# Attention scores of two heads: from split fp32r products to fp32 products issued side by side

## The chip, the cores and the metric

The kernel runs on one core of one Trainium2 chip. The metric is the device time of one execution in microseconds (us); lower is better. Before the change it is 4169.76 us, the median of 3 runs (4169.47 to 4173.31).

## What is computed

Two layers of an encoder with 1024 tokens of width 1024. Each layer makes one wide projection of its input, runs three token mixers on parts of it (RWKV-7, pooling, dilated-window attention), projects and gates their outputs, merges them and normalises. The change lies in the attention mixer, cut here to what matters:

```python
def attention_branch(q, k, v, z, cos, sin):
    q = apply_rope(hd(q), cos, sin)          # 12 heads of 64
    k = apply_rope(hd(k), cos, sin)
    for g, (window, dilation) in enumerate(((128, 1), (512, 4), (2048, 16))):
        # four heads per group; query t sees keys t + j * dilation, |j| <= 64
        s = einsum('...qc,...kc->...qk', q, k) * 64 ** -0.5, masked
        o = softmax(s) @ v, and the log of the softmax denominator
    # the three groups are combined by their denominators, then gated by silu(z)
```

All inputs are fp32.

## The kernel before, in words

**Numbers in two parts.** The large products run on fp32r operands. An fp32 matrix is kept as a high part (its fp32r copy) and a low part (the exact rest), and one product becomes three: high x high, low x high, high x low (lines 584 to 586). These are called dense products here; each has 512 columns.

**The attention stage** (`attention`, from line 1340 on) handles q, k and v in six tiles `ct` of 128 rows: two heads of 64 in each, head 0 in rows 0 to 63 and head 1 in rows 64 to 127. The order is 4, 5, 2, 3, 0, 1. Tiles 4 and 5 belong to dilation group 2, tiles 2 and 3 to group 1, tiles 0 and 1 to group 0. For each tile three dense projections make raw q, k and v. ACT evacuates them (`qkv_evac`, line 1370). `rope` then rotates q and k in place: a DMA makes the shifted copy, DVE multiplies twice (lines 1388 and 1392) and adds (line 1395). `vtrans` transposes v on TensorE (line 1434).

**Units.** A tile's scores are cut into units (`blocks`): in groups 0 and 1 four units of two blocks, 128 queries by 256 keys; in group 2 two units of four blocks, 128 by 128. `unit` makes four steps for one head of a unit: t1 the score products into one PSUM buffer and their scaling and masking by DVE (line 1480); t2 the row minimum on DVE (line 1485) and the exponentials on ACT (line 1488); t3 four transposes and a copy by ACT (lines 1496 and 1500); t4 the products with v and a copy by DVE (lines 1507 and 1511), then a DMA of the output.

**Score products before.** In group 2 (line 1472) a block is one fp32 product of q and k, in the head's own 64 rows. In groups 0 and 1 `parts` (lines 1400 to 1424) first makes, for both heads of a unit, fp32r copies of q and k on ACT (lines 1414, 1416 and 1418: six instructions) and the rests on DVE (lines 1421 and 1423: four). The high part of q stands in the head's rows and its rest in the other head's rows, so that one product over all 128 rows (line 1476) gives high x high and low x high. A second one over the head's 64 rows (line 1477) adds high x low:

```python
nc.tensor.matmul(ps[:, i, :], lhsT=qs, rhs=ks[:, h, o:o + kw], start=True, stop=False)
nc.tensor.matmul(ps[:, i, :], lhsT=qs[hs], rhs=kl[hs, o:o + kw], start=False, stop=True)
```

**What sets the order.** The instructions of the stage are issued by a planner (`Sched.run`) while the program is built. Every step (`Th`) carries assumed times on its engines (P TensorE, D DVE, A ACT, G POOL, S the DMA queue), the steps it needs and the PSUM rings it takes. Streams are given in order of priority: rope, the parts, v's transposes, the units of head 0, the units of head 1, the combine step in two streams, the preparation of the RWKV output, and last the dense products, which fill TensorE whenever nothing else can start. The planner fixes the order in each engine's queue; on the chip the engines then wait for each other by semaphores. Assumed times are, for example, 3000 ns for rope's DMA and 1160 ns for each of its three DVE steps, 2700 ns (A) and 1500 ns (D) for the parts, and for t1 436 ns (P) in groups 0 and 1 and 860 ns in group 2, each with 600 ns (D).

**PSUM rings.** The ring "m" (pool `psm`) has two buffers. Score products, v's transposes and the combine step share them. The transposes of t3 and the products of t4 have buffers of their own for each head. Dense products use ring "d", two buffers.

The RWKV stage is not touched. Its score step (line 979) matters as an example: it issues fp32 products of 64 rows by 64 columns of the array, alternating between the two heads' rows and two PSUM buffers.

Of the kernel before, what the change touches and what calls it, by code (L numbers as in the profile page):

```python
# [10 lines left out]
F32 = mybir.dt.float32  # L11
F32R = mybir.dt.float32r
# [3 lines left out]
ALU = mybir.AluOpType  # L16
# [4 lines left out]
DEPTH, S, D = 2, 1024, 1024  # L21
# [84 lines left out]
KP, SPL, RX, AT = 4, 1, 3, 1  # L106
YA, MA, FA, FP_, BP, RS = 0, 1, 1, 1, 0, 1
DA = 12670.0
SB = 2
DUO, DUOP = 2, -2e9  # L110
ORD = "simop"
LOG = None
# [271 lines left out]
def trunk(ctx: ExitStack, tc: tile.TileContext, a: dict, out, dbg=None):  # L384
    nc = tc.nc
# [5 lines left out]
    psm = ctx.enter_context(tc.tile_pool(name="psm", bufs=2, space=PSUM))  # L391
# [3 lines left out]
    tt = nc.vector.tensor_tensor  # L395
    stt = nc.vector.scalar_tensor_tensor
# [25 lines left out]
    att = dr.tile([1024, 3, 4, 66], F32, name="att")  # L422
# [914 lines left out]
    def attention(l, och, ocl, gr):  # L1337
        P = pc["P"]
        w_in = a["w_in"][l]
        with ExitStack() as es:  # L1340
# [56 lines left out]
                          Th(f3, [("D", 1160.0)], gives=[("rope", n, ct)])]  # L1397
                return o

            def parts(ct, u, bl, prev):  # L1400


                hs = (slice(0, 64), slice(64, 128))
                q0, k0, k1 = bl[0][0], bl[0][1], bl[-1][1] + 256

                def fn():
                    q, k = J["q", ct][:, q0:q0 + 256], J["k", ct][:, k0:k1]
                    qs = a2.tile([128, 2, 256], F32R, tag="qs", name="qs", bufs=SB)
                    ks = a2.tile([128, 2, 384], F32R, tag="ks", name="ks", bufs=SB)
                    kl = a2.tile([128, 384], F32R, tag="kl", name="kl", bufs=SB)  # L1410
                    w = slice(0, k1 - k0)
                    J["parts", ct, u] = qs, ks, kl
                    for h in range(2):
                        nc.scalar.copy(qs[hs[h], h, :], q[hs[h]])
                    for h in range(2):
                        nc.scalar.copy(ks[hs[h], h, w], k[hs[h]])
                    for h in range(2):
                        nc.scalar.copy(ks[hs[1 - h], h, w], k[hs[h]])
                    yield
                    for h in range(2):  # L1420
                        tt(out=qs[hs[1 - h], h, :], in0=q[hs[h]], in1=qs[hs[h], h, :], op=ALU.subtract)
                    for h in range(2):
                        tt(out=kl[hs[h], w], in0=k[hs[h]], in1=ks[hs[h], h, w], op=ALU.subtract)
                return [Th(fn, [("A", 2700.0), ("D", 1500.0)], needs=[("rope", "q", ct), ("rope", "k", ct)] + prev, gives=[("parts", ct, u)])]

            def vtrans(ct, slot, dil, prev):
                offs = VO if dil == 1 else list(range(0, 1024, 128))
                o = []
# [28 lines left out]
                        us.append(([(128 * b, 128 * b, [b]) for b in range(4 * u, 4 * u + 4)], bcm(am3, 4), 128))  # L1457
                return us

            def unit(ct, slot, h, u, spec, first, last):  # L1460
                g = ct // 2
                hg = 2 * (ct % 2) + h
                bl, mask, kw = spec
                nb = len(bl)
                hs = slice(64 * h, 64 * h + 64)
                L = {}

                def t1():
                    ps = psm.tile([128, nb, kw], F32, tag="m", name="pssc")
                    for i, (q0, k0, vi) in enumerate(bl):  # L1470
                        if g == 2:
                            nc.tensor.matmul(ps[:, i, :], lhsT=J["q", ct][hs, q0:q0 + 128], rhs=J["k", ct][hs, k0:k0 + kw], start=True, stop=True)
                        else:
                            qs, ks, kl = J["parts", ct, u]
                            qs, o = qs[:, h, q0 - bl[0][0]:q0 - bl[0][0] + 128], k0 - bl[0][1]
                            nc.tensor.matmul(ps[:, i, :], lhsT=qs, rhs=ks[:, h, o:o + kw], start=True, stop=False)
                            nc.tensor.matmul(ps[:, i, :], lhsT=qs[hs], rhs=kl[hs, o:o + kw], start=False, stop=True)
                    yield
                    L["s"] = s = a2.tile([128, nb, kw], F32, tag=f"s{h}", name="s")
                    stt(out=s, in0=ps, scalar=-0.125, in1=mask, op0=ALU.mult, op1=ALU.subtract)  # L1480

                def t2():
                    s = L["s"]
                    L["o"] = o_ = a2.tile([128, nb, 66], F32, tag=f"o{h}", name="o_")
                    nc.vector.tensor_reduce(out=o_[:, :, 65], in_=s, axis=AX.X, op=ALU.min)
                    yield
                    for i in range(nb):
                        act(s[:, i, :], s[:, i, :], AF.Exp, scale=-1.0, bias=o_[:, i, 65:66])

                def t3():  # L1490
                    s = L["s"]
                    ps = pst.tile([128, 4, 128], F32, tag=f"t{h}", name="pspt")
                    n = 0
                    for i in range(nb):
                        for k in range(kw // 128):
                            nc.tensor.transpose(ps[:, n, :], s[:, i, 128 * k:128 * k + 128], ident)
                            n += 1
                    yield
                    L["p"] = p = a2.tile([128, 4, 128], F32, tag=f"p{h}", name="p")
                    nc.scalar.copy(p, ps)  # L1500

                def t4():
                    ps = pss.tile([128, nb, 65], F32, tag=f"sq{h}", name="pspv")
                    n = 0
                    for i, (q0, k0, vi) in enumerate(bl):
                        for k, x in enumerate(vi):
                            nc.tensor.matmul(ps[:, i, :], lhsT=L["p"][:, n, :], rhs=vts[slot][:, x, h, :], start=(k == 0), stop=(k == len(vi) - 1))
                            n += 1
                    yield
                    o_ = L["o"]  # L1510
                    nc.vector.tensor_copy(o_[:, :, 0:65], ps)
                    if g == 0:
                        nc.gpsimd.dma_start(out=att[256 * u:256 * u + 256, g, hg, :].rearrange("(b p) c -> p b c", p=128), in_=o_)
                    elif g == 1:
                        nc.gpsimd.dma_start(out=att[:, g, hg, :].rearrange("(b p r) c -> r p b c", r=4, p=128)[u], in_=o_)
                    else:
                        for rr in range(2):
                            nc.gpsimd.dma_start(out=att[:, g, hg, :].rearrange("(i b r) c -> r i b c", b=8, r=2)[rr][:, 4 * u:4 * u + 4],
                                                in_=o_[64 * rr:64 * rr + 64])
                nd = [("parts", ct, u)] if g < 2 else [("rope", "q", ct), ("rope", "k", ct)]  # L1520
                return [Th(t1, [("P", 860.0 if g == 2 else 436.0), ("D", 600.0)], needs=nd, ring=("m",), gives=[("t1", ct, u, h)]),
                        Th(t2, [("D", 602.0), ("A", 800.0)]), Th(t3, [("P", 428.0), ("A", 478.0)]),
                        Th(t4, [("P", 432.0), ("D", 200.0)], needs=[("vt", ct)] if first else (), gives=[("attu", ct, h, u)] + ([("att", ct, h)] if last else []))]

            def combine(t):
                L = {}
# [39 lines left out]
                        Th(c4, [("P", 430.0), ("D", 330.0), ("A", 300.0), ("D", 300.0)], ring=("m",), needs=[("szc", 0), ("szc", 1)])]  # L1566

            dense, ro, vt, un, cb = [], [Th(ld_c, [("S", 200.0)], needs=[("raw", "q", order[0])])], [], [[], []], []
            sp, done = [], []
            for n, ct in enumerate(order):  # L1570
                dil = DIL[ct // 2]
                prev = [("att", order[n - 2], h) for h in range(2)] if n >= 2 else []
                for nm, base in (("q", QC), ("k", KC), ("v", VC)):
                    col = base // 128 + ct
                    nd = prev if nm != "v" else ([("vt", order[n - 1])] if n >= 1 else [])
                    dense += dn.tile(w_in[:, col * 128:(col + 1) * 128], 8, xr, qkv_evac(nm, ct, col, dil), needs=nd, gives=[("raw", nm, ct)], key=(col, l))
                ro += rope(ct, dil)
                vt += vtrans(ct, n % 2, dil, prev)
                us = blocks(ct // 2)
                for u, spec in enumerate(us if ct < 4 else ()):  # L1580
                    sp += parts(ct, u, spec[0], [done[-SB] + (h,) for h in range(2)] if len(done) >= SB else [])
                    done.append(("t1", ct, u))
                for h in range(2):
                    for u, spec in enumerate(us):
                        un[h] += unit(ct, n % 2, h, u, spec, u == 0, u == len(us) - 1)
            for i in range(2):
                col = ZC // 128 + i
                dense += dn.tile(w_in[:, col * 128:(col + 1) * 128], 8, xr, szc_evac(i), gives=[("szc", i)], ev=(("A", 1140.0), ("D", 600.0)))
# [23 lines left out]
            oap = sum((oa_part(n) for n in range(16)), [])  # L1612
            dn.more = es.enter_context(tc.tile_pool(name="wraw", bufs=2)), len(dn.pieces)
            hint(l, PB // 128, PB // 128 + 1)
            sc.run([ro, sp, vt, un[0], un[1], cbs[0] + cbs[2] + cbs[4] + cbs[6], cbs[1] + cbs[3] + cbs[5] + cbs[7], oap, dense])
            dn.more = None


# [371 lines left out]
```

## Time and profile before

| | |
|---|---|
| median of the runs | 4169.76 us (4169.47 to 4173.31, 3 runs) |
| the profiled execution's own time | 4178.51 us |
| its span, first to last instruction | 4176.7 us, mean granted TensorE clock 0.983 |
| busy: TensorE, weight loads, DVE, ACT, POOL | 96%, 74%, 58%, 55%, 39% |

In the rows below PE is TensorE's matmuls, PEld its weight loads, DVE the vector engine, ACT the scalar engine, POOL GpSimd. Times are in us from the span's start. Matmuls are pipelined, so each is shown longer than its share of the queue; the distance from one start to the next is what it costs. The granted clock is 1.0 or 0.50 in any one moment; a mean between them is a mix.

### The profile page before, as it was taken

The numbers are of one execution on the slowest core, as the hardware profiler recorded it, in microseconds if no ns is written. First come the engines' busy times: TensorE is split into PE (matmuls) and PEld (weight loads), VectorE is DVE, ScalarE is ACT, GpSimd is POOL, SyncE is SP. The second block draws the span as 40 slices with busy tenths as digits, with TensorE's granted clock in tenths as the row PEclk, the third lists the DMA queues.
The fourth block names the chain that finished last, engine by engine and source line by source line (L and its number), as shares of the span: only waits on it lengthen the run. The fifth ranks groups of instructions, "written<-read, shape, count | busy, mean of one in ns | idle before, by whom it ended". The sixth has DMA issues, their size and how long they took to land. (4 is left out here: it accounts for less than half of the span.)

```text
span 4176.7 us, 120866 instructions
## 1 busy us (share of the span) xinstructions
PE 4002.9 (96%) x51576; PEld 3102.3 (74%) x51576; DVE 2409.4 (58%) x4361; ACT 2303.7 (55%) x4582; POOL 1648.9 (39%) x2498
## 2 busy tenths in 40 slices
PE   8999999999999999999989999999999999999998
PEld 6677777777777778877766777777777777788777
DVE  3776776666524555545647667766665245555455
ACT  4677777767643553322146777777777344533210
POOL 3343445443433333353233444444334333334532
PEclk9999999999999899999999999999999998999999
DMA  2111111111124333155311111111111243321553
GB/s 89 31 47 44 40 44 47 40 44 46 55 83 116 113 105 99 55 174 184 125 51 31 49 40 43 47 42 42 44 51 53 85 119 108 113 88 55 188 178 117
DMA packets 329194, 326.42 MB, mean 78 GB/s; under 512 B 23536, under 2 KB 264384, under 8 KB 328655
## 3 DMA queue, kind: packets, MB, share of 16 engines
q1 hardware_dynamic: 301551, 233.66, 18.8%
q0 software_dynamic: 27104, 85.04, 5.8%
q8 instruction: 404, 6.62, 0.7%
q14 instruction: 135, 1.11, 0.1%
HBM read 224.86 MB, written 81.99 MB: 73 GB/s over the span
## 5 line engine op out<-in xcount | busy, mean ns | idle before, releaser
L584 PE MATMUL psdn<-xh,wh 128*128 128x512 f32 x3136 | 1337.1, 426 | 11.2 <-ACT wh L552 9.2
L586 PE MATMUL psdn<-xh,wl 128*128 128x512 f32 x3136 | 1242.8, 396 | 10.2 <-POOL wl L553 10.2
L585 PE MATMUL psdn<-xl,wh 128*128 128x512 f32 x3136 | 1239.0, 395 | 0.0
L553 POOL TENSOR_TENSOR wl<-wr,wh 128x512 fp32r<-128x512 f32 (+1 forms) x436 | 591.7, 1358 | 1353.7 <-ACT wh L552 1327.5
L584 PEld LDWEIGHTS psdn<-xh,wh 128*128 128x128 f32 x3136 | 595.7, 190 | 172.4 <-issue 25.5
L586 PEld LDWEIGHTS psdn<-xh,wl 128*128 128x128 f32 x3136 | 595.7, 190 | 153.0 <-POOL wl L553 18.6
L585 PEld LDWEIGHTS psdn<-xl,wh 128*128 128x128 f32 x3136 | 597.9, 191 | 101.1 <-issue 4.8
L552 ACT CAST wh<-wr 128x512 fp32r<-128x512 f32 (+2 forms) x484 | 290.3, 600 | 641.3 <-PE psdn L585 295.6
L1060 ACT CAST U<-pst 64x512 f16<-64x512 f32 x768 | 445.0, 579 | 115.8 <-PE pst L1055 98.8
L1088 DVE TENSOR_TENSOR X<-pst,c 128x512 f16<-128x512 f32 x320 | 219.5, 686 | 197.0 <-PE pst L1055 196.7
L1186 DVE SCALAR_TENSOR_TENSOR sbd<-sqp,wc,sbd 128x64 f32<-128x64 f32 x480 | 113.8, 278 | 215.8 <-PE sqp L1181 156.9
L1166 ACT COPY uv<-sqp 64x128 f32<-64x128 f32 x512 | 132.0, 258 | 85.3 <-PE sqp L1162 77.2
L1155 ACT ACTIVATE sbd<-sbd,wc 128x64 f32<-128x64 f32 x480 | 140.4, 340 | 43.6 <-PE sqp L1147 31.1
L1055 PEld LDWEIGHTS <-X 64*64 64x64 f16 x6144 | 144.1, 107 | 25.5 <-DVE sc L984 8.0
L1072 POOL TENSOR_TENSOR nl<-sc,nh 64x512 f16<-64x512 f32 x128 | 154.7, 1209 | 8.3 <-ACT nh L1069 3.1
L1055 PE MATMUL pst<-U,X 64*64 64x64 f16 x5120 | 153.6, 197 | 2.2 <-ACT U L1060 0.9
L1162 PEld LDWEIGHTS sqp<-u,sc 64*64 64x64 f32 x2048 | 80.1, 133 | 91.6 <-issue 51.3
L979 PE MATMUL pssc<-ar,nk 64*64 64x128 f32 x4096 | 146.4, 274 | 0.4
L1055 PEld LDWEIGHTS <-U 64*64 64x64 f16 x5120 | 113.1, 109 | 44.9 <-ACT uv L1166 14.7
L1055 PE MATMUL pst<-X,U 64*64 64x64 f16 x5120 | 140.3, 194 | 0.4
L1151 DVE TENSOR_TENSOR u<-sqp,sc 128x128 f32<-128x128 f32 x256 | 73.5, 287 | 112.7 <-PE sqp L1147 60.1
L1144 PEld LDWEIGHTS sqp<-sbd,ar 64*64 64x64 f32 x2048 | 83.6, 133 | 73.8 <-issue 43.2
(716 smaller groups left out, 7977.5 us busy)
## 6 DMA issues: line engine op xcount, KB each, us to landing
wr<-in_w_in_dram SPq DMA_DIRECT2D x360, 256.0 KB, 2.9
sga<-gt POOLq DMA_DIRECT2D x96, 256.0 KB, 2.3
g<-sga SPq DMA_DIRECT2D x96, 256.0 KB, 4.6
wr<-in_proj_a_dram SPq DMA_DIRECT2D x64, 256.0 KB, 3.4
sza<-sz POOLq DMA_DIRECT2D x32, 256.0 KB, 3.1
bva<-bv POOLq DMA_DIRECT2D x32, 256.0 KB, 2.7
oa<-o POOLq DMA_DIRECT2D x32, 256.0 KB, 3.3
oat<-oa SPq DMA_DIRECT2D x32, 256.0 KB, 4.4
```

The costliest lines, as they stand in the source:

```text
L552: nc.scalar.copy(hi[:, 0:n, :], r[:, 0:n, :])
L553: self.lo.tensor_tensor(out=lo[:, 0:n, :], in0=r[:, 0:n, :], in1=hi[:, 0:n, :], op=ALU.subtract)
L584: nc.tensor.matmul(ps, lhsT=hi[:, kk, :], rhs=ah, start=(k == 0), stop=False)
L585: nc.tensor.matmul(ps, lhsT=hi[:, kk, :], rhs=al, start=False, stop=False)
L586: nc.tensor.matmul(ps, lhsT=lo[:, kk, :], rhs=ah, start=False, stop=(k == nk - 1))
L979: nc.tensor.matmul(ps[h][HS[h if x == 0 else 1 - h], c, :], lhsT=nk[HS[h], c, x, :], rhs=ar[HS[h], c].rearrange("p a t -> p (a t)"), start ...
L1055: nc.tensor.matmul(ps[HS[1 - h if mir else h], d, c], lhsT=l, rhs=r, start=start and d == 0 and c == 0, stop=stop, skip_group_check=True)
L1060: nc.scalar.copy(dst[HS[h]], ps[HS[1 - h]])
L1072: nc.gpsimd.tensor_tensor(out=nl[HS[h]], in0=sc[HS[h], :, :, h, 0:64], in1=nh[HS[h]], op=ALU.subtract)
L1088: tt(out=x, in0=ps[0], in1=mask(i + 1), op=ALU.mult)
L1155: act(sbd[d], sbd[d], AF.Copy, scale=J["wc", d, Q % NB][:, pl[d][0]:pl[d][0] + 1])
L1166: nc.scalar.copy(uv[HS[h], two, h, :], pu[HS[h], 128:256].rearrange("p (s e) -> p s e", s=2))
```

## The change

The exact parts are gone: `parts`, its stream `sp` and the bound `SB` on its buffers. In all groups a score product is one fp32 product of q and k as rope leaves them, in the head's own 64 rows. The step t1 now belongs to both heads of a unit: it takes both buffers of ring "m", one for each head, and issues for each block the product of head 0 and then that of head 1. DVE then scales and masks head 0's buffer, which is given back at once, and head 1's. All t1 steps form one stream `t1s`, in the place of the parts' stream; a t1 step needs rope of q and k of its tile and the t4 steps of both heads of the unit two before. The steps t2, t3 and t4 are unchanged, move to `rest` and stay in the streams of head 0 and head 1; t2 needs its unit's t1. Units are now made unit by unit with both heads inside. In groups 0 and 1 the score instructions have 64 rows and 256 columns, in group 2 64 rows and 128 columns as before.

```diff
-            def parts(ct, u, bl, prev):
...
-                    for h in range(2):
-                        nc.scalar.copy(qs[hs[h], h, :], q[hs[h]])
-                    for h in range(2):
-                        nc.scalar.copy(ks[hs[h], h, w], k[hs[h]])
-                    for h in range(2):
-                        nc.scalar.copy(ks[hs[1 - h], h, w], k[hs[h]])
-                    yield
-                    for h in range(2):
-                        tt(out=qs[hs[1 - h], h, :], in0=q[hs[h]], in1=qs[hs[h], h, :], op=ALU.subtract)
-                    for h in range(2):
-                        tt(out=kl[hs[h], w], in0=k[hs[h]], in1=ks[hs[h], h, w], op=ALU.subtract)
...
-            def unit(ct, slot, h, u, spec, first, last):
+            def unit(ct, slot, u, spec, first, last):
...
+                def t1():
+                    ps = [psm.tile([128, nb, kw], F32, tag="m", name="pssc") for _ in range(2)]
+                    q, k = J["q", ct], J["k", ct]
+                    for i, (q0, k0, vi) in enumerate(bl):
+                        for h in range(2):
+                            nc.tensor.matmul(ps[h][:, i, :], lhsT=q[hs[h], q0:q0 + 128], rhs=k[hs[h], k0:k0 + kw], start=True, stop=True)
+                    for h in range(2):
+                        yield None if h == 0 else "first"
+                        S_[h] = a2.tile([128, nb, kw], F32, tag=f"s{h}", name="s")
+                        stt(out=S_[h], in0=ps[h], scalar=-0.125, in1=mask, op0=ALU.mult, op1=ALU.subtract)
+                t1s.append(Th(t1, [("P", 880.0), ("D", 600.0), ("D", 600.0)], ring=("m", "m"), gives=[("t1", n)],
+                              needs=[("rope", "q", ct), ("rope", "k", ct)] + ([("t4", n - 2, h) for h in range(2)] if n >= 2 else [])))
+                for h in range(2):
+                    un[h] += rest(ct, slot, h, u, spec, first, last, S_, n)
...
-                nd = [("parts", ct, u)] if g < 2 else [("rope", "q", ct), ("rope", "k", ct)]
-                return [Th(t1, [("P", 860.0 if g == 2 else 436.0), ("D", 600.0)], needs=nd, ring=("m",), gives=[("t1", ct, u, h)]),
-                        Th(t2, [("D", 602.0), ("A", 800.0)]), Th(t3, [("P", 428.0), ("A", 478.0)]),
-                        Th(t4, [("P", 432.0), ("D", 200.0)], needs=[("vt", ct)] if first else (), gives=[("attu", ct, h, u)] + ([("att", ct, h)] if last else []))]
+                return [Th(t2, [("D", 602.0), ("A", 800.0)], needs=[("t1", n)]), Th(t3, [("P", 428.0), ("A", 478.0)]),
+                        Th(t4, [("P", 432.0), ("D", 200.0)], needs=[("vt", ct)] if first else (),
+                           gives=[("t4", n, h), ("attu", ct, h, u)] + ([("att", ct, h)] if last else []))]
...
-            sc.run([ro, sp, vt, un[0], un[1], cbs[0] + cbs[2] + cbs[4] + cbs[6], cbs[1] + cbs[3] + cbs[5] + cbs[7], oap, dense])
+            sc.run([ro, t1s, vt, un[0], un[1], cbs[0] + cbs[2] + cbs[4] + cbs[6], cbs[1] + cbs[3] + cbs[5] + cbs[7], oap, dense])
```

## Rows read from the trace of the kernel before

**Rows 1.** The page: the span, and busy time with share and instructions.

```profile
span 4176.7 us, 120866 instructions
PE 4002.9 (96%) x51576; PEld 3102.3 (74%) x51576; DVE 2409.4 (58%) x4361; ACT 2303.7 (55%) x4582; POOL 1648.9 (39%) x2498
```

**Rows 2.** Busy time by stretch (length, engines, clock, DMA): attention stage, both layers.

```profile
1268.00:1627.00 359.00, 351.30 (x1747) 283.06 (x1748) 193.22 (x327) 172.50 (x349) 123.97 (x128) 0.96 0.40 114
3347.00:3706.00 359.00, 351.35 (x1748) 283.39 (x1749) 194.26 (x328) 172.32 (x349) 124.64 (x129) 0.96 0.40 115
```

**Rows 3.** Waits of PE, 1225 to 1640 us: total, times, longest.

```profile
PE pssc L1472 <- DVE rawk L1395: 5.5, 2, 2.9
PE psv L1434 <- ACT rawv L1370: 1.9, 1, 1.9
PE pspt L1496 <- ACT s L1488: 1.7, 1, 1.7
PE psdn L584 <- ACT rawv L1370: 0.7, 1, 0.7
...
PE psv L1434 <- DVE s L1480: 0.2, 1, 0.2
```

**Rows 4.** Busy time by stretch, as in rows 2; the clock stands third from the end.

```profile
1365.80:1376.00 10.20, 10.20 (x26) 7.01 (x25) 4.79 (x9) 5.37 (x13) 1.80 (x3) 0.50 0.25 79
1423.80:1437.40 13.60, 13.02 (x39) 9.99 (x40) 6.83 (x13) 6.99 (x16) 4.58 (x5) 0.50 0.21 65
1270.20:1273.60 3.40, 3.40 (x9) 2.63 (x10) 2.10 (x4) 2.28 (x6) 0.31 (x1) 0.50 0.00 0
1313.00:1327.00 14.00, 11.31 (x74) 9.76 (x75) 6.40 (x9) 5.98 (x14) 3.50 (x4) 1.00 0.37 118
```

**Rows 5.** Timeline of PE (start, duration): one head's scores, group 1.

```profile
1382.82 0.39 PE L585 MATMUL psdn<-xl,wh 128*128 128x512 f32 x1
1383.05 0.40 PE L586 MATMUL psdn<-xh,wl 128*128 128x512 f32 x1
...
1383.49 0.38 PE L1477 MATMUL pssc<-kl,qs 64*128 64x256 f32 x1
1383.80 0.38 PE L1476 MATMUL pssc<-ks,qs 128*128 128x256 f32 x1
...
1384.76 0.40 PE L585 MATMUL psdn<-xl,wh 128*128 128x512 f32 x1
```

**Rows 6.** Timeline of PE: both heads' scores of a unit, group 2.

```profile
1281.33 0.40 PE L586 MATMUL psdn<-xh,wl 128*128 128x512 f32 x1
1281.65 1.71 PE L1472 MATMUL pssc<-rawk,rawq 64*128 64x128 f32 x16
...
1283.63 0.40 PE L585 MATMUL psdn<-xl,wh 128*128 128x512 f32 x1
```

**Rows 7.** Line 1472 alone by stretch: length, PE busy (records), PEld busy, clock, DMA.

```profile
1281.65:1282.20 0.55, 0.55 (x4) 0.55 (x5) 1.00 0.64 108
1282.20:1282.54 0.34, 0.34 (x9) 0.34 (x8) 1.00 0.16 25
```

**Rows 8.** Timeline of PE: RWKV scores, and what starts behind them.

```profile
622.18 1.10 PE L979 MATMUL pssc<-ar,nk 64*64 64x128 f32 x32
623.10 0.42 PE L1055 MATMUL pst<-U,X 64*64 64x64 f16 x16
```

**Rows 9.** Timeline of ACT: a copy of k's parts, idle time and releaser in brackets.

```profile
1361.49 0.83 ACT L1416 CAST ks<-rawk 64x256 fp32r<-64x256 f32 x2 [2.08 <-DVE rawk L1395]
```

**Rows 10.** Timeline of DVE: rope's first step on k, tiles 4, 2 and 0.

```profile
1262.33 3.00 DVE L1388 TENSOR_TENSOR rawk<-rawk,cos 128x1024 f32<-128x1024 f32 x1 [4.42 <-ACT wh L552]
1355.55 2.67 DVE L1388 TENSOR_TENSOR rawk<-rawk,cos 128x1024 f32<-128x1024 f32 x1 [4.26 <-DMA rot<-rawk]
1476.83 1.23 DVE L1388 TENSOR_TENSOR rawk<-rawk,cos 128x1024 f32<-128x1024 f32 x1 [5.48 <-DMA rot<-rawk]
```

More of the change, by code (lines that the diff above doesn't have):

```diff
@@ L108 @@
 DA = 12670.0
-SB = 2
 DUO, DUOP = 2, -2e9
@@ L1398, in rope @@
                 return o
-            def parts(ct, u, bl, prev):
[L1403 to L1412, printed above, removed]
-                    for h in range(2):
-                        nc.scalar.copy(qs[hs[h], h, :], q[hs[h]])
-                    for h in range(2):
-                        nc.scalar.copy(ks[hs[h], h, w], k[hs[h]])
-                    for h in range(2):
-                        nc.scalar.copy(ks[hs[1 - h], h, w], k[hs[h]])
-                    yield
-                    for h in range(2):
-                        tt(out=qs[hs[1 - h], h, :], in0=q[hs[h]], in1=qs[hs[h], h, :], op=ALU.subtract)
-                    for h in range(2):
-                        tt(out=kl[hs[h], w], in0=k[hs[h]], in1=ks[hs[h], h, w], op=ALU.subtract)
-                return [Th(fn, [("A", 2700.0), ("D", 1500.0)], needs=[("rope", "q", ct), ("rope", "k", ct)] + prev, gives=[("parts", ct, u)])]
             def vtrans(ct, slot, dil, prev):
@@ L1458, in blocks, with rest @@
                 return us
-            def unit(ct, slot, h, u, spec, first, last):
+            def unit(ct, slot, u, spec, first, last):
+                g = ct // 2
+                bl, mask, kw = spec
+                nb = len(bl)
+                hs = (slice(0, 64), slice(64, 128))
+                S_ = {}
+                n = len(t1s)
+                def t1():
[12 more added lines that the diff above has]
+                    un[h] += rest(ct, slot, h, u, spec, first, last, S_, n)
+            def rest(ct, slot, h, u, spec, first, last, S_, n):
                 g = ct // 2
@@ L1464, in unit @@
                 nb = len(bl)
-                hs = slice(64 * h, 64 * h + 64)
                 L = {}
[L1468 to L1480, printed above, removed]
                 def t2():
-                    s = L["s"]
+                    L["s"] = s = S_[h]
                     L["o"] = o_ = a2.tile([128, nb, 66], F32, tag=f"o{h}", name="o_")
@@ L1568, in attention @@
             dense, ro, vt, un, cb = [], [Th(ld_c, [("S", 200.0)], needs=[("raw", "q", order[0])])], [], [[], []], []
-            sp, done = [], []
+            t1s = []
             for n, ct in enumerate(order):
@@ L1579, in attention @@
                 us = blocks(ct // 2)
[L1580 to L1585, printed above, removed]
+                for u, spec in enumerate(us):
+                    unit(ct, n % 2, u, spec, u == 0, u == len(us) - 1)
             for i in range(2):
```

## The prediction

> **What bounds the kernel now.** I read the page first: TensorE (PE) is busy 96% of the span [rows 1]. A busy PE need not be a PE at its peak, so I then looked at the two stretches that the change touches, one in each layer, from the first score product of the attention stage to its end. There PE is busy 351 of 359 us and the others far less: DVE 193, ACT 173, POOL 124 [rows 2]. The stage is limited by PE, so its length goes by the time that PE's instructions take up in its queue, plus PE's waits, plus the time at the lower clock. The waits of PE over the first of these stretches come to about 10 us: 5.5 for rope's last add of k, 1.9 and 0.7 for evacuations of v, 1.7 for an exponential on ACT [rows 3]. The mean granted clock is 0.96 [rows 2]; since a stretch has either 1.0 or 0.50 (2.4 or 1.2 GHz), that is about 8% of 359 us, some 28 us a layer, at half. Two stretches hold most of it: 10.2 us from 1365.8 and 13.6 us from 1423.8, both at 0.50 [rows 4]. Each began at one of the waits just named: the 1.9 us wait for v (1363 to 1365), and the 1.7 us wait for the exponential.
>
> **The part that is removed: score products with exact parts.** At full clock one head's scores of one unit are four products of 256 columns. From the start of the dense product ahead of them to the second dense product behind them 1383.05 to 1384.76 = 1.71 us pass [rows 5]. Two starts of dense products lie 0.23 us apart there (1382.82 to 1383.05), so 1.71 - 2 x 0.23 = 1.25 us is what the scores take from the queue, with the slow entry and exit in it; a unit of two heads costs 2.50 us.
>
> **The part that is added: fp32 products of both heads.** The nearest rows are the scores of the other head group, which are fp32 already: from 1281.33 to 1283.63, 2.30 us, less 0.46 us for the two dense products, 1.84 us for 16 records [rows 6]. These are 8 products (4 blocks, 2 heads), so one fp32 product leaves two records, here of 128 columns. They are issued head after head. Yet the records are not in single file: 4 of them touch the first 0.55 us, 9 the next 0.34 us, where the first head ends and the second begins [rows 7]. So the products of rows 0 to 63 and of rows 64 to 127 run at the same time whenever both are at hand. The scores of the RWKV stage, whose products alternate between heads, rows and banks, show it in full: 32 records of 128 columns from 622.18 to 623.10, 0.92 us [rows 8], which is eight rounds of four at 0.115 us.
>
> With 0.115 us for a record of 128 columns, the 16 records of [rows 6], of which about three ran beside others, fill 13 x 0.115 = 1.50 us, and 1.84 - 1.50 = 0.34 us is the price of entering and leaving. For 256 columns no row shows an fp32 record. The bounds are 0.115 us (no dearer than 128 columns) and 0.31 us (the spacing of the 256-column products that go, 1383.49 to 1383.80 [rows 5]). I take twice 0.115, 0.23 us, because a record that streams twice the columns takes twice the time and a dense record of 512 columns has 0.23 us too. A unit then has 8 records in four rounds of two: 4 x 0.23 + 0.34 = 1.26 us.
>
> Saved: 2.50 - 1.26 = 1.24 us a unit, and 4 tiles x 4 units x 2 layers = 32 units: **39.7 us**. The bounds give 32 x (2.50 - 0.80) = 54 and 32 x (2.50 - 1.58) = 29 us. The fp32 group gains only the alternation: 8 rounds x 0.115 + 0.34 = 1.26 us in place of 1.84, in 2 tiles x 2 units x 2 layers = 8 units: **4.6 us**. Together 44 us.
>
> **ACT and DVE.** Six copies and four subtractions a unit leave ACT and DVE. I cost that at nothing: PE is the limit, and ACT and DVE are busy about half of the stage [rows 2]. What they can give back are waits: at 1361.49 ACT's copies of k stood 2.08 us for rope's last add [rows 9], the evacuation of v queued behind them, and PE's 1.9 us wait for v followed.
>
> **The wait that is added.** The scores of a tile now follow rope directly. The planner allows rope's shift DMA 3.0 us and each of three DVE steps 1.16 us; the trace has 3.00, 2.67 and 1.23 us for the first step alone in three tiles [rows 10]. In the first two tiles, where the scores already follow rope, PE waited 5.5 us in two waits [rows 3]. If the four other tiles do the same, two at 2.7 us and two, with the shorter steps, at about 1.7 us, that is 8.8 us a layer in place of 4.3 (1.9 + 1.7 + 0.7): 4.5 us more, **9 us** in both. Behind a waiting score product stand the dense products of PE's queue and all that evacuates them. Bounds: nothing, and 4 x 2.9 - 4.3 = 7.3 us a layer, 15 us.
>
> **The clock.** Of 28 us a layer at half clock half is lost, 14 us. The two long stretches held score products in which PE waited between records, and their triggers go. The first two tiles' waits for rope, 5.5 us in two [rows 3], left one stretch of 3.4 us and none (0.50 from 1270.2, 1.00 from 1313) [rows 4]. With the six waits I expect some 18 us at half: 5 us a layer won, **9 us** in both. Bounds: 14 us a layer won, or up to 10 us a layer lost if each new wait drags 12 us at half clock behind it (4 x 12 = 48 against 28).
>
> **Two banks at once.** A score step takes both buffers of the PSUM ring that it shares with the transposes of v and the combine step; a wait for DVE to empty them is bounded by nothing and by two evacuations. PE's waits for such an evacuation were 0.2 us [rows 3]; I take nothing.
>
> The sum: 44 - 9 + 9 = **44 us** of the profiled execution's 4178.5 us (span 4176.7 and 1.8 around it), which is 8.7 us above the median of the runs, 4169.8. Against the median: **4126 us**.
>
> **The rivals.**
> - *The waits go and no new ones come*, as ACT and DVE are free: 44 + 2 x 4.3 + 2 x 7 to 14 = 67 to 80 us, about 4100. For it: both long half-clock stretches begin at a queue that the removed copies held up. Against it: the two rope waits that are there already.
> - *Rope's waits are paid in full, at half clock*: 44 - 15 - 20 = 9 us, about 4161. Against it: one of the two waits of that kind left no half clock at all.
> - *Records strictly in order*: if no record may start ahead of one issued before it, the two records of one product can't both run beside the other head's, and a unit's four rounds become five: 32 x 0.23 = 7 us less gained, about 4133. Against it: 9 records touch 0.34 us [rows 7], so the second head's began before the first's were out. The Trainium skill states that order, for matmuls' starts and ends ("TensorE: Matmul & The Clock Gate", Part 3, "What overlaps and what doesn't"); by its rule the time is 4133, by the rows 4126.
> - *Heads in single file* (the change doesn't do what it says): 8 x 0.23 + 0.34 = 2.18 us a unit, 32 x 0.32 = 10 us, about 4160. [Rows 7, 8] speak against it.
> - *Slower: the double bank*. Each of 40 score steps waits at the head of PE's queue until DVE, behind a rope step of 2.7 to 3.0 us [rows 10], has emptied both banks. It decides from 44/40 = 1.1 us a step; at two evacuations and one such step queued, some 2.2 us, 88 us are lost: 4170 + 44 = 4214.
>
> **How the numbers follow.** The forecast 0.50, waits gone 0.20, records in order 0.08, rope paid in full 0.11, single file 0.05, double bank 0.06. The range leaves out the better part of the second case and most of the fourth and the last: 4093 to 4156. About 0.2% (8 us) is what a measurement here can tell from no change. All cases but the last are faster; the fourth and fifth clear the 8 us so narrowly that I put 0.05 of their 0.16 within it: faster 0.89, within 0.05, slower 0.06.
>
> **What would show it.** Right: score records of the two heads starting together, a unit's eight records in about 1 us, the 32 units no longer above 1.3 us; stretches [rows 2] shorter by about 22 us each. Wrong: PE waits at a score product that are ended by a subtraction-and-scale on DVE (the double bank), by rope above 3 us each, more half clock than 28 us a layer, or dense products that have run out before the units are done, so that PE idles near the stage's end.

## The result, and the profile after the change

The median fell from 4170.74 us (4169.47 to 4173.31, 4 runs) to 4115.67 us (4110.03 to 4116.77, 4 runs): ratio 0.9855, 95% interval 0.9842 to 0.9868, or 55 us. The forecast was 44 us less and 4126 us. The profiled execution after took 4110.03 us with a span of 4107.9 us; it is the fastest of its four, as the profiled one before was slow for its kernel, so the two spans differ by more (69 us) than the medians. What follows is therefore read from the attention stage alone, from its first score product to the first evacuation of the pooling stage, in both layers.

Busy time by stretch, that stage before (both layers), columns as in [rows 2]:

```profile
1268.40:1648.30 379.90, 372.60 (x1841) 300.65 (x1842) 194.50 (x330) 177.15 (x357) 131.36 (x138) 0.96 0.39 113
3347.30:3727.00 379.70, 372.32 (x1842) 300.67 (x1843) 195.43 (x330) 176.97 (x357) 132.00 (x138) 0.96 0.39 113
```

The same stage after the change:

```profile
1263.60:1613.90 350.30, 340.56 (x1841) 281.07 (x1842) 164.55 (x266) 137.99 (x261) 134.66 (x138) 0.99 0.42 122
3306.80:3659.30 352.50, 342.48 (x1842) 281.94 (x1843) 164.03 (x266) 137.79 (x262) 136.53 (x138) 0.99 0.42 121
```

It is 29.6 and 27.2 us shorter, 56.8 us in all: the whole of the gain. PE still fills it. ACT and DVE lost 39 and 30 us a layer. PE's work can be added up from the starts in the trace: each record counts up to the next one's start, waits of more than 0.1 us are left out and time at half clock counts half. From the first evacuation of q to the stage's end, both layers, the score products then take 86.7 us before and 42.6 us after, and everything else that PE does there 677.5 and 678.1 us. There are 384 score records in either kernel; what changed is that those of the two heads run at once.

The score products of a unit of group 1, both heads, timeline of PE (start, duration):

```profile
1357.16 0.39 PE L585 MATMUL psdn<-xh,wl 128*128 128x512 f32 x1
1357.48 1.14 PE L1447 MATMUL pssc<-rawk,rawq 64*128 64x256 f32 x8
1358.54 0.50 PE L583 MATMUL psdn<-xh,wh 128*128 128x512 f32 x1
1358.88 0.40 PE L584 MATMUL psdn<-xl,wh 128*128 128x512 f32 x1
```

From 1357.16 to 1358.88 are 1.72 us; less the two dense products' 0.46 us that is 1.26 us for two heads, where [rows 5] gave 1.25 us for one. In group 2 the same reading is 1268.21 to 1269.96, 1.75 - 0.46 = 1.29 us, where [rows 6] gave 1.84:

```profile
1268.21 0.39 PE L585 MATMUL psdn<-xh,wl 128*128 128x512 f32 x1
1268.53 1.16 PE L1447 MATMUL pssc<-rawk,rawq 64*128 64x128 f32 x16
...
1269.96 0.39 PE L584 MATMUL psdn<-xl,wh 128*128 128x512 f32 x1
```

PE's waits (total, times, longest), in layer 0; they answer to [rows 3]:

```profile
PE pssc L1447 <- DVE rawk L1394: 12.7, 6, 3.0
PE psdn L585 <- POOL wl L552: 0.4, 1, 0.4
```

The waits for v and for the exponential are gone. Rope's last add of k is waited for in all six tiles, 12.7 us in layer 0 and 12.8 us in layer 1, where before it was 5.5 us in two tiles. (The stage begins at its first score product and so leaves out the wait that ends there, 2.5 to 3.4 us in most kernels below and under 0.9 us with rope due later; all sums of waits count it. Counted from the first evacuation of q, with that wait inside, the stages before and after differ by 56.7 us, much the same.) The half clock of [rows 4] has shrunk to short stretches: 3.4 us twice in layer 0, three times in layer 1, for example

```profile
1407.10:1410.40 3.30, 3.30 (x10) 2.17 (x9) 2.48 (x4) 0.04 (x1) 1.77 (x2) 0.50 0.51 164
```

0.7 us behind the end, at 1406.39, of a wait for rope. Over both layers the granted clock stood at half for 54.6 us of the stage before and 17.1 us after (added up from its changes in the trace; the means 0.96 and 0.99 above say the same more coarsely).

So the 56.8 us divide as follows: half clock, (54.6 - 17.1)/2 = 18.8 us won; PE's waits of more than 0.1 us, 20.4 before and 25.5 after, 5.1 us lost; what is left, 43.1 us, is the score products, where 32 x (2.50 - 1.26) + 8 x (1.84 - 1.29) = 44.1 us were to be had by the timelines.

### The profile page after: what moved, and what is told of

It reads as the page before. It is cut to its first block, busy times and chain, and to the rows that moved or that the text cites. A ratio compares the mean times of both kernels' runs of the same rounds, so it can differ in the third digit from the quotient of the medians.

```text
span 4107.9 us, 120670 instructions
## 1 busy us (share of the span) xinstructions
PE 3933.5 (96%) x51576; PEld 3060.1 (74%) x51576; DVE 2344.7 (57%) x4233; ACT 2224.0 (54%) x4390; POOL 1653.9 (40%) x2498
## 5 line engine op out<-in xcount | busy, mean ns | idle before, releaser
L1154 ACT ACTIVATE sbd<-sbd,wc 128x64 f32<-128x64 f32 x480 | 140.3, 340 | 43.1 <-PE sqp L1146 30.6
```

The costliest lines, as they stand in the source:

```text
L1154: act(sbd[d], sbd[d], AF.Copy, scale=J["wc", d, Q % NB][:, pl[d][0]:pl[d][0] + 1])
```

## Experiments

Four questions were open: whether the products overlap because they alternate, whether the removed parts or the split products made the half clock, what the joint step by itself is worth, and whether the waits for rope stand on the path. The table gives all kernels that were run; the stage is that of both layers, the waits are PE's of more than 0.1 us, with the one that ends at the first score product, and the last columns are a unit's price as read above. Stage, waits and half clock come from one profiled execution of each kernel. The ratios in the text go by executions of the kernel before taken alongside (medians 4173.4 and 4172.7 us).

| kernel | median us | stage us | PE waits us | half clock us | unit, groups 0 and 1 | unit, group 2 |
|---|---|---|---|---|---|---|
| before | 4170.7 | 759.6 | 20.4 | 54.6 | 2.50 | 1.84 |
| after | 4115.7 | 702.8 | 25.5 | 17.1 | 1.26 | 1.29 |
| head by head | 4127.1 | 711.9 | 27.1 | 27.3 | 1.28 | 1.84 |
| parts made, unused | 4112.3 | 696.6 | 19.9 | 3.4 | 1.26 | 1.29 |
| split products, joint step | 4138.4 | 729.7 | 16.0 | 10.2 | 2.51 | 1.29 |
| rope due later | 4086.1 | 671.9 | 2.8 | 0 | 1.26 | 1.29 |
| before, rope due later | 4155.2 | 737.3 | 11.7 | 17.1 | 2.50 | 1.84 or apart |
| split, joint, rope due later | 4131.8 | 719.7 | 5.8 | 6.8 | 2.51 | 1.29 |
| fp32, heads apart | 4138.3 | 726.4 | 27.8 | 27.3 | 1.28 or 2.52 | 1.84 |
| rope due later, head by head | 4091.3 | 677.5 | 3.4 | 0 | 1.28 | 1.84 |
| rope due later, two by two | 4084.5, one run | 673.8 | 4.2 | 0 | 1.28 | 1.38 |

### The order inside a step

```diff
-                    for i, (q0, k0, vi) in enumerate(bl):
-                        for h in range(2):
+                    for h in range(2):
+                        for i, (q0, k0, vi) in enumerate(bl):
```

> Only the order of the score products inside a step is changed: all blocks of head 0, then all of head 1; the planner's order is the same. Theory (the products overlap because neighbours in the queue use different rows): little overlap is left where the heads meet. If nothing overlaps, a unit of groups 0 and 1 takes 8 x 0.22 + 0.35 = 2.1 us in place of 1.27, 32 units lose 27 us, the 8 units of group 2 lose 0.55 us each, 4 us: 4116 + 31 = 4147. Rival (TensorE looks some records ahead by itself, as it did in group 2 before, where the second head began about four records before the first ended): with four records a head nearly one round in five is lost, 32 x 0.22 + 4 = 11 us: 4127.

Measured 4127.1 us, ratio to before 0.9887 (0.9872 to 0.9901), so 11 us above the changed kernel, the rival's number. But it is not made as the rival made it. In groups 0 and 1 a unit costs the same in either order. Timeline of PE, this kernel, a unit of group 1, and one of group 2:

```profile
1363.92 0.40 PE L585 MATMUL psdn<-xh,wl 128*128 128x512 f32 x1
1364.25 1.14 PE L1447 MATMUL pssc<-rawk,rawq 64*128 64x256 f32 x8
...
1365.66 0.39 PE L584 MATMUL psdn<-xl,wh 128*128 128x512 f32 x1
...
1268.62 0.40 PE L585 MATMUL psdn<-xh,wl 128*128 128x512 f32 x1
1268.95 1.71 PE L1447 MATMUL pssc<-rawk,rawq 64*128 64x128 f32 x16
...
1270.92 0.39 PE L584 MATMUL psdn<-xl,wh 128*128 128x512 f32 x1
```

1365.66 - 1363.92 - 0.46 = 1.28 us, against 1.84 us in group 2. Line 1447 alone, in the first tenth of a microsecond of that unit of group 1 (PE busy and records, PEld, clock, DMA):

```profile
1364.20:1364.30 0.10, 0.05 (x2) 0.05 (x2) 1.00 0.00 0
```

Two records have begun. Records of one head stand 0.21 us or more apart (four of a lone head take 1.06 us in the run with the heads apart, below), so they are one of each head, although the first head's other three stand between them in the queue. Only group 2, with eight records a head, loses: 8 x 0.55 = 4.4 us. The rest of the stage's 9.1 us is half clock, at most (27.3 - 17.1)/2 = 5.1 us, and 1.6 us of waits, together 2 us more than the stage shows. The order does not set these by itself, as the same pair of kernels without waits shows (this edit together with that of the run with rope due later, below):

> The changed kernel with rope due later and the products head by head inside a step. Without waits the clock no longer hides the price of the order. Theory (TensorE takes the second head up to four records ahead, so only group 2, with eight records a head, loses): 8 units x 0.55 = 4.4 us more than 4086: 4090. Rival (the order cost 11 us in the first such run because of the products): 4097.

Measured 4091.3 us against 4086.1; the stage is 677.5 against 671.9 us, 5.6 us more, with 0.6 us more waits and no half clock in either; by their starts the score products take 4.6 us more. The theory's 4.4 us holds, within what these runs can tell.

To see how far ahead the second head may stand, the blocks were issued two of one head, then two of the other, also with rope due later (a single execution):

```diff
-                    for i, (q0, k0, vi) in enumerate(bl):
-                        for h in range(2):
+                    for i, h in [(2 * c + j, h) for c in range(nb // 2) for h in range(2) for j in range(2)]:
+                            q0, k0, vi = bl[i]
```

> The changed kernel with rope due later; inside a step two blocks of head 0 are issued, then two of head 1, and so on. Groups 0 and 1 are as in the run head by head. In group 2 the second head's first product now stands four records behind the first head's first. Theory (TensorE takes records of the other rows up to about four records ahead): both heads run together all the time, a unit of group 2 takes 1.09 us from its first record to the next dense product, as alternating, not 1.64 as head by head. Rival (records of one head that stand in one row block the other at each change): 1.3 us or more.

Timeline of PE, a unit of group 2 in this kernel:

```profile
1264.81 0.39 PE L585 MATMUL psdn<-xh,wl 128*128 128x512 f32 x1
1265.12 1.26 PE L1447 MATMUL pssc<-rawk,rawq 64*128 64x128 f32 x16
...
1266.65 0.39 PE L584 MATMUL psdn<-xl,wh 128*128 128x512 f32 x1
```

1266.65 - 1264.81 - 0.46 = 1.38 us, between the two: 0.09 us more than alternating, about one record's 0.11 us. The second head runs beside the first with three records between, and the unit takes nine rounds in place of eight. Neither expectation had that.

### fp32 products, the heads apart

The kernel before, with one fp32 product a block in all groups and no parts, but with each head's step by itself:

```diff
-                        if g == 2:
+                        if True:
...
-                nd = [("parts", ct, u)] if g < 2 else [("rope", "q", ct), ("rope", "k", ct)]
+                nd = [("rope", "q", ct), ("rope", "k", ct)]
...
-                for u, spec in enumerate(us if ct < 4 else ()):
+                for u, spec in enumerate(()):
```

> The kernel before without parts: in all groups one fp32 product a block, but each head's score step by itself, in its own place in the queue, with one buffer, as before. Theory (the gain needs the two heads next to each other in the queue; fp32 by itself gains nothing): a head apart costs 4 x 0.22 + 0.34 = 1.2 us against 1.25, some 3 us over both layers; waits for rope in six tiles add 5 us, the clock gives back 0 to 20: 4153 to 4173. Rival (the planner puts the heads next to each other anyway, as in group 2 before): 4120 to 4135.

Measured 4138.3 us, between the two: the planner put the two heads next to each other in 24 of the 32 units and apart in 8. Where they are apart, one head is seen alone. Timeline of PE:

```profile
1390.30 0.40 PE L586 MATMUL psdn<-xh,wl 128*128 128x512 f32 x1
1390.62 1.13 PE L1472 MATMUL pssc<-rawk,rawq 64*128 64x256 f32 x4
...
1392.02 0.39 PE L585 MATMUL psdn<-xl,wh 128*128 128x512 f32 x1
```

1392.02 - 1390.30 - 0.46 = 1.26 us for one head, what two cost in the changed kernel, and within 0.01 us what one cost with split products. So an fp32 product by itself gains nothing, and the second head is free once it is a neighbour, also without the joint step. Against the changed kernel this stage is 23.6 us longer: 8 x 1.26 = 10 us for heads apart, 8 x 0.55 = 4 us in group 2, 5 us of half clock, 2 us of waits, 22 us together.

### Parts made but not read

The parts stream is put back, its results unread; a score step of groups 0 and 1 waits for it.

```diff
...
+                    if ct < 4:
+                        sp += parts(ct, u, spec[0], [("t1", len(t1s) - SB)])
...
-                              needs=[("rope", "q", ct), ("rope", "k", ct)] + ...
+                              needs=([("rope", "q", ct), ("rope", "k", ct)] if ct > 3 else [("parts", ct, u)]) + ...
```

> The products stay fp32 and side by side; the parts stream of before is made again (copies on ACT, subtractions on DVE) and a score step of groups 0 and 1 waits for it, but nothing reads the parts. Scores still 1.27 us a unit. Theory (the long half-clock stretches of before came from PE waiting behind the parts in ACT's queue): the waits for v and for the exponential return, 4 us a layer in place of the 7 us that the four later tiles wait for rope, and half clock goes from 7 to 10 us a layer back to some 25: 4116 + 2 x (8 - 3) = 4126. Rival (the split products themselves, with their gaps, kept the clock low): half clock stays near 10 us a layer and the waits alone change, 4110 to 4118.

Measured 4112.3 us, ratio 0.9853 (0.9839 to 0.9868): the rival's range, and no slower than without the parts. Its waits and its busy time:

```profile
PE pssc L1474 <- DVE rawk L1395: 5.4, 2, 2.7
PE psv L1434 <- ACT rawv L1370: 2.1, 1, 2.1
```

```profile
1262.40:1611.40 349.00, 341.62 (x1841) 279.35 (x1842) 197.01 (x330) 175.79 (x357) 133.86 (x138) 1.00 0.43 123
```

ACT is back at 176 us and DVE at 197, and the 2.1 us wait for v is back, but no long half clock follows it. ACT's and DVE's share of the change is worth nothing that the medians show. It is not nothing to the last microsecond: the stage has 5.6 us less waits and 6.8 us less loss at half clock than after, yet is only 6.2 us shorter, so some 6 us more went into PE's queue, about half of it at the transposes of t3; why is open. The theory that the parts in ACT's queue by themselves made the half clock is out.

### The joint step with split products

The same kernel with the parts read: the two fp32r products of before take the place of the fp32 product in groups 0 and 1.

```diff
+                            if g == 2:
                                 nc.tensor.matmul(ps[h][:, i, :], lhsT=q[hs[h], q0:q0 + 128], rhs=k[hs[h], k0:k0 + kw], start=True, stop=True)
+                            else:
...
+                                nc.tensor.matmul(ps[h][:, i, :], lhsT=qs, rhs=ks[:, h, o:o + kw], start=True, stop=False)
+                                nc.tensor.matmul(ps[h][:, i, :], lhsT=qs[hs[h]], rhs=kl[hs[h], o:o + kw], start=False, stop=True)
```

> The structure of the changed kernel (one score step for both heads, two buffers, one stream), with the parts and the two fp32r products of before in groups 0 and 1; group 2 stays fp32 side by side. Theory (nearly the whole gain is the cheaper products): a unit takes about 2.5 us again, 32 x 1.24 = 40 us, and the clock gives back its 10 us a layer: 4116 + 40 + 10 to 20 = 4166 to 4176. Rival (a good part comes from the joint step and the priorities): 4140 to 4155.

Measured 4138.4 us, ratio 0.9923 (0.9906 to 0.9939): far below the theory's range and 2 us under the rival's. The products cost what they did, 1368.32 - 1365.35 - 0.46 = 2.51 us a unit. Timeline of PE:

```profile
1365.35 0.40 PE L586 MATMUL psdn<-xh,wl 128*128 128x512 f32 x1
1365.59 0.28 PE L1479 MATMUL pssc<-ks,qs 128*128 128x256 f32 x1
...
1368.32 0.39 PE L585 MATMUL psdn<-xl,wh 128*128 128x512 f32 x1
```

The stage is 26.9 us longer than after: 32 x 1.25 = 40 us of products, less 9.5 us of waits (16.0 against 25.5), less 3.4 us of half clock. And it is 29.9 us shorter than before, with the same parts and the same products: (54.6 - 10.2)/2 = 22.2 us of that is half clock, 4.4 us waits, 4.4 us group 2. The wait for v is there in both layers, and layer 1 has no half clock at all:

```profile
PE psv L1434 <- ACT rawv L1370: 2.3, 2, 2.0
```

```profile
3325.10:3687.70 362.60, 357.40 (x1842) 291.06 (x1843) 196.70 (x330) 176.41 (x358) 136.00 (x138) 1.00 0.41 118
```

So parts and split products are not enough to make the long half-clock stretches of before; the order in which the steps stand counts. But the joint step is not the only way to be rid of them: the run with the heads apart, which has separate steps and neither parts nor split products, has no stretch above 6.8 us. Stretches of 10 us and more occur only where split products stand in separate steps.

The parts of the gain do not add up, then. From the kernel before, the joint step with split products gives 35 us, and fp32 products in separate steps give 34 us, of which most are the 24 units whose heads became neighbours; together they give 55 us, since both give back some of the same half clock (22.2 and 13.7 us alone, 18.8 us together).

### Rope due later

The planner's assumed time for rope's DMA of k is raised; the instructions stay the same.

```diff
-                    o += [Th(f0, [("S", 3000.0)], needs=[("raw", n, ct)]), ...
+                    o += [Th(f0, [("S", 3000.0 + (0.0 if n == "q" else 3000.0 if ct > 1 else 1000.0))], needs=[("raw", n, ct)]), ...
```

> The changed kernel, with the planner's assumed time of the DMA of rope of k at 6000 ns in tiles 5 to 2 and 4000 ns in tiles 1 and 0 in place of 3000; the instructions are the same. Theory (PE's waits for rope stand on the path, since dense products could run in their place): the 12.7 us of waits a layer fall to about 1, and the half clock behind them goes: 4116 - 2 x 11.5 - 2 x 3 to 4 = 4085 to 4090. Rival (the work only moves: the units end later and PE idles or the next stage waits for the combine step): within 5 us of 4116.

Measured 4086.1 us (4079.6 to 4091.5), ratio to before 0.9791 (0.9776 to 0.9806): the theory's 4085 to 4090, and a version that beats both kernels by plain planning. Waits of PE and busy time in layer 0:

```profile
PE psdn L585 <- POOL wl L552: 0.5, 1, 0.5
PE pssc L1447 <- DVE rawk L1394: 0.3, 1, 0.3
PE pspv L1489 <- ACT p L1482: 0.3, 1, 0.3
```

```profile
1265.60:1600.60 335.00, 334.44 (x1828) 275.35 (x1828) 163.18 (x266) 135.97 (x260) 134.13 (x138) 1.00 0.43 128
```

PE is busy 334 of 335 us at full clock. Against the changed kernel the stage lost 30.9 us: 25.5 - 2.8 = 22.7 us of waits and 17.1/2 = 8.6 us of half clock (counted from the first evacuation of q it lost 30.1 us). The score products now stand behind dense products that used to stand behind them: the first starts at 1265.64 us in place of 1263.61, without its wait of 3.0 us.

The same edit in the kernel before, and with split products in the joint step:

> The kernel before, with the planner's assumed time of rope's DMA of k raised as in the run with rope due later (6000 ns in tiles 5 to 2, 4000 ns in 1 and 0). Scores stay 1.25 us a head. Theory (half clock in this stage needs a wait of PE, and the waits come from rope being late against the plan, directly or through ACT's queue): waits fall from 20 us in both layers to about 4, half clock from 55 us to under 10: 4172 - 16 - 23 = 4133. Rival (the parts in ACT's queue hold up v and the exponentials by themselves): only the rope waits of the first two tiles go, 4172 - 11 - 3 = 4158.

Measured 4155.2 us, ratio 0.9962 (0.9948 to 0.9975): by the number the rival, but of another make: half clock fell from 54.6 to 17.1 us, most of the way to the theory's 10, while 11.7 us of waits stayed, most of them for v and the exponential on ACT. By stage time the run explains itself to 5 us (8.7 of waits and 18.8 of half clock won, 22.3 in all); 3 of the 5 are group 2, where 4 units now have their heads apart; the rest is open.

> The joint score step with the parts and the split products, with rope due later. With no waits and no half clock left, the difference to the changed kernel with rope due later is the price of the products alone: 32 units x (2.51 - 1.27) = 40 us, so 4086 + 40 = 4126 and some 5 us below the kernel before with rope due later (group 2 side by side). Rival (waits and clock still differ): 4105 to 4115, as the runs without the later rope differed by 23 us only.

Measured 4131.8 us: 46 us above the changed kernel with the same edit, where 40 was expected. The stage is 47.8 us longer: 40 us of products, 3.0 us of waits, 3.4 us of half clock. The products' price is thus the same with waits and without, to within 2 us.

## Why the prediction was right

- **Score products.** The core of the sum, 1.24 us a unit of groups 0 and 1 and 0.58 of group 2, was measured as 1.24 and 0.55. The step that carried it, from [rows 7, 8] to two heads in the time of one, is shown by the timeline after and by the lone head of the run with the heads apart. A 256-column record at twice the 128-column one (0.23 us) was nearly right: 1.26 us a unit was forecast and measured, but the starts are 0.21 to 0.22 us apart, and entering and leaving cost about 0.06 us more than the 0.34 us taken, so that two small errors cancel. What the reason left open is when both heads are "at hand", as I put it: in groups 0 and 1 it is enough that the heads are neighbours, and in group 2, with eight records of one head in front, it is not.
- **Records strictly in order.** By this rival a unit would have had five rounds; it has four, since its eight records take 1.06 us (1357.48 to 1358.54), as long as the four of a lone head (1390.62 to 1391.68). The Trainium skill's rule that matmuls start and end strictly in program order ("TensorE: Matmul & The Clock Gate", Part 3, "What overlaps and what doesn't") does not agree with this trace: in the run head by head the second head's first record began within 0.1 us of the first head's, with three records of the first between.
- **ACT and DVE at nothing.** Right: with the parts made again the median is the same (4112.3 against 4115.7 us), though waits, half clock and PE's queue then differ by some us each.
- **The wait that was added.** Right in kind, too large in size: four new waits of about 2.8, 2.7, 0.8 and 0.8 us in place of 2.7, 2.7, 1.7 and 1.7. The last two tiles waited half of what I took from their shorter rope steps: 5.1 us in both layers, not 9.
- **The clock.** The term that was mis-sized: I expected "some 18 us at half" a layer and 9 us won; it was 7 and 10 us a layer and 18.8 us won. I let each new wait drag half clock behind it as the two old ones had. I also wrote that in the two long stretches PE waited between records; [rows 4] don't show that, with PE busy 10.20 of 10.20 us in the first. The runs show that a wait of 2.0 to 2.1 us for v can leave no half clock at all, with parts and split products alike, so the long stretches of before came with the order of the work around the waits. Which feature of that order is decisive was not tried, so the cause behind the 18.8 us stays open in part. What is shown is that the long stretches are gone with the joint step (split products or not) and also with fp32 products in separate steps, and that with less than 5 us of waits in both layers there is no half clock in the stage (three kernels).
- **The rivals.** "The waits go and no new ones come" was wrong on the waits and right on the clock (14 to 28 us in both layers), so the result lies between it and the forecast. The double bank never showed: no wait of PE for DVE's scaling stands in the profile after. Heads in single file did not occur in any unit after; the nearest thing is the 8 units of the run with the heads apart, 2.52 us, with dense products between the heads and so with the entry paid twice.

Against the stage's 56.8 us the sum of 44 was thus short by 10 us in the clock and by 4 us in the waits, and long by 1 us in the scores. The two large misses have the same sign, so no lucky cancelling brought the forecast near; the clock's share of the gain was forecast at half its size.

## What to carry to other kernels

Two products that each use half of the array's rows cost one, if they stand near each other in TensorE's queue; here they also wrote different PSUM buffers, and one buffer for both was not tried. A slower number format can then be as cheap as a split one, and its preparation goes. Price such a change from the start-to-start distances of the queue, not from durations. When PE waits for a step that the plan believed done, ask first what the plan assumes for it: raising one assumed DMA time gave 30 us more, over half of what the rewrite gave.

## What the runs showed of the hardware that was not expected

- A record of the other row half is started although three records of the first half stand ahead of it in the queue; in a two-by-two order about one record's time is lost (1.38 against 1.29 us), and with eight records of one half in front the overlap is down to about three records (1.84 us).
- An fp32r product of 256 columns stands 0.31 us from the next in the mixed sequence of 128-row and 64-row products (the first of them, behind a dense product of 128 rows, 0.21 us), while a dense one of 512 columns stands 0.23 us. Whether the columns or the change of rows costs that was not tried.
- Waits of like length left between nothing and 14 us of half clock behind them: 1.7 us went with 13.6 us [rows 3, 4], while behind one of 2.8 us (ended at 1354.15 in the changed kernel) the clock stayed at 1.00:

```profile
1354.00:1366.00 12.00, 11.85 (x74) 9.65 (x75) 5.54 (x11) 5.47 (x11) 3.62 (x4) 1.00 0.30 86
```
